# A fused two-block transformer kernel in fp32: the modulation products handed out differently between VectorE and TensorE

## Chip, cores, metric

One core of one Trainium2 chip runs the whole program. The metric is the device time of one execution in microseconds (us). A profiled execution gives the trace from which all rows below are taken.

## What is computed

The reference runs two blocks, one after the other, on x of 256 tokens by 2048 channels, all in fp32. In outline:

```
c_act = silu(c)
for l in 0, 1:                                         # first block
    shift, scale, gate = split(c_act @ w_mod[l] + b_mod[l], 3)
    h = x * (1 + scale) + shift
    l == 0:  y = diff_attention(h)                     # 8 heads
    l == 1:  k, v, F = shared_kv(x * (1 + scale_kv) + shift_kv)   # from c_act @ w_mod_kv
             y = forgetting_attention(h, k, v, F)      # 16 heads
    x = layer_norm(alpha * x + gate * y)
# second block: S5 mixer, then a squared-ReLU MLP of 8192
sh1, sc1, gt1, sh2, sc2, gt2 = split(silu(c_2) @ w_mod_2 + b_mod_2, 6)
csh1, csc1, ... = split(silu(c_ctx_2) @ w_mod_2 + b_mod_2, 6)
h_ctx, h_lat = modulate(rmsnorm(ctx), csh1, csc1), modulate(rmsnorm(x), sh1, sc1)
y = glu(gelu(s5_two_directions(h_ctx -> initial state, h_lat)))
x = x + gt1 * rmsnorm(y)
x = x + gt2 * rmsnorm(relu(modulate(rmsnorm(x), sh2, sc2) @ w1)**2 @ w2)
```

The products c @ w_mod are the subject here: a vector times a matrix of 2048 rows and 2048 columns per shift, scale or gate. All their weights are read once.

## The kernel before

**Big products.** Activations lie transposed (channels on the partitions). A weight block of 2048 by 128, called a unit here, comes in two halves of 0.5 MB; ScalarE rounds each half to `wh` (L134) and VectorE subtracts to get the rest `wl` (L135). A unit is then 48 matmuls on TensorE: `pj` in `mm_t` (L163 to L165), `pjv` in `mm_n` (L200 to L202). The MLP uses `mm_w` with 32 matmuls (L176, L177). `weights()` hands out one unit, and prepares two ahead.

**Modulation products.** `gemv` (L207) splits each 2048 by 2048 product into two halves of the columns and each half into eight chunks. A chunk is two loads `graw` of 512 KB (L268, on SP's queue, four buffers). It is used in one of two ways. On VectorE ("dve") each load is multiplied by its 128 values of c and added to the accumulator `gacc` (L237; the first load of a half by ScalarE, L235), and at the end of the half four matmuls L246 sum the partitions. On TensorE ("pe") a chunk is eight small matmuls into `g` (L222), which the trace shows as 16 records. Both ends go through L249 to L257. Products for two vectors at once (`mc`) always go to TensorE.

**Who decides.** The chunks wait in one list: m0 (layer 0), mk (keys and values), m1 (layer 1), mc (shift and scale of the S5 layer, for c_2 and the context), m1_2, m2_2 (S5's gate), m2_4, m2_3, m2_5 (MLP). Each call of `weights()` calls `bg()`, which takes the next entry of the stage's policy: "dve", "pe" or None. The policies are `P_L0A` (heads 0 to 3 of layer 0), `POL0` (heads 4 to 7), `P_ON0` (its output product), `P_KV`, `P_QG` (queries and gates of layer 1), `P_ON1` (its output product), `P_GLU`, `P_MLP`. Besides, `BG_M` chunks go to TensorE ahead of the S5 scan and `BG_V` after each of the first `BG_B` S5 blocks. Where an accumulator is still open at the start of the S5 layer, its half is finished on VectorE:

```
        while self.open:
            self.bg(1, "dve")
            self.bg_use(0)
```

`start_ctx` starts the states of the context (`ctx_states`, tile `ctx_ws`) as soon as mc is done; they are a side job in steps between units.

**Order on each engine.** A list scheduler writes the order of each engine from the program's order and its own model of the engines, so that an instruction can stand earlier than in the code when its input is expected early. On the chip each engine keeps that order. So a chunk asked for in the MLP can stand in VectorE's row ahead of the MLP's own inputs. Those inputs are `residual` (L1599, L1600), `xn` (L1612) and the split of `h` (L420), from which TensorE's first MLP matmuls start; four MLP units run interleaved there as the 16 pieces of `h` come. The keys' stage begins in the same way with `norm` (L1112, L1113) and the split `kL` (L420).

Of the kernel before, what the change touches and what calls it, by code (L numbers as in the profile page):

```python
# [47 lines left out]
KO_J = 4  # L48
KO_K = 8
P_START = ("pe",)  # L50
P_L0A = ('dve', 'pe')
P_KV = ('dve', 'pe')
P_QG = ('dve', 'dve', 'pe')
P_W = ("pe",)
P_GLU = ('dve',)
P_MLP = ('dve', None, None)
P_ON0 = ('dve', 'dve', 'dve', None)
P_ON1 = ('pe', 'dve', None)
BG_V = 5
BG_W = 0  # L60
PF_N = 6
ZT = 'm'
# [11 lines left out]
DVE_V = 3  # L74
POOL_V = tuple(range(5))
BG_M = 12
BG_B = 0
TL = True
KTS = 1
ENG = {'m0': 'dve', 'mc': 'pe', 'mk': 'dve', 'm1': 'dve', 'm2': 'pe'}  # L80
HOLD = 0
E_K = "x"
X_GLU = (0,)
X_KV = (0,)
# [5 lines left out]
X_QG = (0,)  # L90
# [16 lines left out]
class K:  # L107
# [185 lines left out]
    def bg(self, n=1, eng=None):  # L293

        for _ in range(n):
            e = eng or next(self.pol)
            if e and self.bgq and not (self.hold and self.bgq[0][0].startswith("m2")):
                name, gen, left = self.bgq[0]
                use = gen.send(ENG[name[:2]] if e == "x" else e)
                self.late.append((name, use))  # L300
                self.bg_use(LATE)
                self.bgq[0] = (name, gen, left - 1)
                if left == 1:
                    self.bgq.pop(0)
# [397 lines left out]
    def run(self):  # L702
        tc, I = self.tc, self.I
        from contextlib import ExitStack
        with ExitStack() as es:
# [21 lines left out]
            self.late = []  # L727
            self.hold = HOLD
            self.steps = itertools.cycle((1,))
# [46 lines left out]
    def V(self, n):  # L776
        i = VEC[n] * KT
        return self.vecs[:, i:i + KT]
# [112 lines left out]
    def layer0(self):  # L891
# [73 lines left out]
        self.side.append(gen)  # L965
        self.policy(P_L0A, X_L0A)
        prev = None
# [150 lines left out]
    def layer1(self):  # L1118
# [52 lines left out]
        kT, v = [], []  # L1171
        self.policy(P_KV, X_KV)
        vgen = self.s5_outputs_table(self.act.tile([128, 4096], F32, name="gen2_ws", tag="act"))
# [74 lines left out]
        def start_ctx():  # L1248
            if self.ctx is None and not self.bg_open("mc_0") and not self.bg_open("mc_1"):
                Sc, Bc = self.small_bg("sc", V("mixpre"), self.mc[1], None, self.mc[0])  # L1250
                self.ctx = self.ctx_states(Sc, Bc)
                self.side.append(self.ctx)
                self.steps = itertools.cycle(P_CTX)

        self.ctx = None
        self.policy(P_QG, X_QG)
        for h in range(16):
            start_ctx()
            ps = self.mm_t(h_)
            nc.scalar.mul(qT, ps, QS)  # L1260
            if h:
                trans()
            ps = self.mm_t(h_)
            if h:
                pv(h - 1)
            t = self.tmp("tg1")
            nc.scalar.activation(t, ps, AF.Tanh, scale=0.5)
            nc.vector.scalar_tensor_tensor(sg, t, 1.0, ps, op0=ADD, op1=MUL)
            scores(h)
        trans()  # L1270
        pv(15)
        for n in ("mc_1", "mc_0", "m1_2"):
            self.bg_finish(n)
        start_ctx()
        self.policy(P_ON1, X_ON1)
        self.norm, self.rb = self.out_norm(lambda kt: o[kt], self.m1[2], 1, rms=True)
# [69 lines left out]
    def s5_mix(self):  # L1346
# [106 lines left out]
        def open_sums(kt, z):  # L1453

            w = self.raw.tile([128, 2 * KO_J, 128], F32, name="wko", tag="raw")
            nc.sync.dma_start(w.rearrange("p j c -> p (j c)"), I["glu0"][kt])
            for j in range(KO_J):
                if kt == 0:
                    ko.append(self.pj.tile([128, 2, T], F32, name="ko", tag="pj"))
                for i in range(2):  # L1460
                    nc.tensor.matmul(ko[j][:, i], w[:, 2 * j + i], z, start=kt == 0 and i == 0, stop=False)
# [3 lines left out]
        for n, b in enumerate(blocks):  # L1465
# [66 lines left out]
            for kt, zh in late:  # L1532
                open_sums(kt, zh)
            if n < BG_B:
                self.bg(BG_V)

# [227 lines left out]
```

## Time and profile before

| what | value |
|---|---|
| median of 3 runs | 2542.77 us (2542.32 to 2544.66) |
| the profiled execution | 2548.22 us, span 2546.4 us |
| instructions | 47968 |
| mean granted TensorE clock | 0.964 of full speed |

The span is what the trace shows; the profiled execution lasts 1.82 us longer than its span. The profiled execution is 5.45 us above the median, so differences in time are worked out within the trace and then set on the median.

### The profile page before, as it was taken

The page shows a single profiled execution, that of the slowest core. Times are in us where ns is not written, and L with a number is a line of the kernel's source. Part 1 is how long each engine was busy: PE and PEld are TensorE (multiplying, and loading weights), DVE is VectorE, ACT ScalarE, POOL GpSimd, SP SyncE. Part 2 cuts the span into 40 slices and gives each one's busy share as a digit, 9 for nine tenths or more (in the row PEclk, how much of TensorE's full clock was granted, in tenths as well). Part 3 has the DMA queues.
Part 4 walks back from the last instruction along what each step waited for, and adds up shares of the span by engine and source line. Part 5 has one row for each costly group of instructions (what it writes and reads, how often), then busy time and mean ns, then how long its engine had stood idle before and what let it go on. Part 6 is the DMA issues. An engine that isn't in the chain of part 4 may idle for free.

```text
span 2546.4 us, 47968 instructions
## 1 busy us (share of the span) xinstructions
PE 2377.1 (93%) x18854; PEld 2051.9 (81%) x18854; DVE 1776.8 (70%) x3360; ACT 1239.5 (49%) x2153; POOL 118.8 (5%) x234
## 2 busy tenths in 40 slices
PE   5699999999899999999998874999899999999997
PEld 1299999999678888988886663898688888888885
DVE  3288778877775555778788997877854565665655
ACT  0554554444365556666653543544544443443442
POOL 0000000000002110000000021000000000000000
PEclk9999999999889999999998886999899999999998
DMA  9999999878769998878786762998366666666652
GB/s 325 339 344 325 323 321 344 306 275 316 265 226 342 327 332 290 296 248 290 257 273 230 233 210 77 334 320 279 118 186 187 186 187 191 189 190 184 189 182 91
DMA packets 203316, 644.66 MB, mean 253 GB/s; under 512 B 41009, under 2 KB 49457, under 8 KB 202705
## 3 DMA queue, kind: packets, MB, share of 16 engines
q1 hardware_dynamic: 195616, 620.47, 72.7%
q0 software_dynamic: 7472, 21.11, 2.1%
q8 instruction: 148, 2.42, 0.4%
q14 instruction: 80, 0.65, 0.1%
HBM read 613.71 MB, written 25.69 MB: 251 GB/s over the span
## 4 chain that ended last, share of the span: by engine, by line
PE 84%; DVE 9%; DMA 3%; ACT 2%; issue 1%; SPq 0%; POOL 0%; DVEq 0%; ACTq 0%; POOLq 0%
PE pj L176 18%; PE pj L163 12%; PE pj L164 12%; PE pj L165 12%; PE pj L177 9%; PE g L222 3%; PE pjv L200 3%; DMA graw<-in_w_mod 3%; PE pjv L201 2%; PE pjv L202 2%; DVE scan_t L1415 2%; DVE scan_t L1417 2%; DVE S L1419 2%; PE inc L697 2%; PE st L370 1%
## 5 line engine op out<-in xcount | busy, mean ns | idle before, releaser
L135 DVE TENSOR_TENSOR wl<-w,wh 128x1024 fp32r<-128x1024 f32 x631 | 770.0, 1224 | 465.2 <-ACT wh L134 457.2
L134 ACT CAST wh<-w 128x1024 fp32r<-128x1024 f32 x632 | 659.1, 1050 | 711.1 <-PE pj L176 283.0
L176 PE MATMUL pj<-h,wh 128*128 128x512 f32 x1024 | 362.9, 399 | 6.8 <-DVE h L420 5.0
L176 PE MATMUL pj<-d,wh 128*128 128x512 f32 x1024 | 360.3, 398 | 0.0
L237 DVE SCALAR_TENSOR_TENSOR gacc<-graw,csilu,gacc 128x1024 f32<-128x1024 f32 x211 | 270.2, 1281 | 27.4 <-DMA graw<-in_w_mod 18.6
L177 PE MATMUL pj<-h,wl 128*128 128x256 f32 x1024 | 287.5, 281 | 1.1 <-DVE wl L135 1.1
L177 PE MATMUL pj<-d,wl 128*128 128x256 f32 x1024 | 285.8, 280 | 0.0
L176 PEld LDWEIGHTS pj<-h,wh 128*128 128x128 f32 x1024 | 193.1, 189 | 55.8 <-issue 4.0
L176 PEld LDWEIGHTS pj<-d,wh 128*128 128x128 f32 x1024 | 192.0, 188 | 48.2 <-PE pj L177 1.7
L163 PE MATMUL pj<-hH,wh 128*128 128x256 f32 x768 | 221.6, 289 | 6.2 <-ACT hH L419 4.0
L165 PE MATMUL pj<-hH,wl 128*128 128x256 f32 x768 | 221.4, 289 | 0.5 <-DVE wl L135 0.5
L164 PE MATMUL pj<-hL,wh 128*128 128x256 f32 x768 | 221.1, 288 | 0.0
L222 PE MATMUL g<-graw,czc 128*32 128x256 f32 x1744 | 168.4, 469 | 49.6 <-DMA graw<-in_w_mod 48.0
L177 PEld LDWEIGHTS pj<-h,wl 128*128 128x128 f32 x1024 | 194.0, 189 | 1.5 <-DVE wl L135 1.5
L177 PEld LDWEIGHTS pj<-d,wl 128*128 128x128 f32 x1024 | 193.1, 189 | 0.4
L163 PEld LDWEIGHTS pj<-hH,wh 128*128 128x128 f32 x768 | 148.8, 194 | 9.8 <-ACT hH L419 4.1
L165 PEld LDWEIGHTS pj<-hH,wl 128*128 128x128 f32 x768 | 148.6, 194 | 4.5 <-issue 3.3
L164 PEld LDWEIGHTS pj<-hL,wh 128*128 128x128 f32 x768 | 148.9, 194 | 3.8 <-issue 3.7
L222 PEld LDWEIGHTS g<-graw,czc 128*32 128x32 f32 x1744 | 46.0, 119 | 129.4 <-DMA graw<-in_w_mod 105.5
L163 PE MATMUL pj<-h1H,wh 128*128 128x256 f32 x512 | 147.1, 290 | 0.3 <-ACT ctx_ws L1323 0.2
L164 PE MATMUL pj<-h1L,wh 128*128 128x256 f32 x512 | 146.4, 287 | 0.0
L165 PE MATMUL pj<-h1H,wl 128*128 128x256 f32 x512 | 146.0, 286 | 0.0
(480 smaller groups left out, 5201.4 us busy)
## 6 DMA issues: line engine op xcount, KB each, us to landing
graw<-in_w_mod SPq DMA_DIRECT2D x384, 512.0 KB, 5.8
w<-in_mlp_in SPq DMA_DIRECT2D x128, 512.0 KB, 4.3
w<-in_mlp_out SPq DMA_DIRECT2D x128, 512.0 KB, 4.3
w<-in_a_in SPq DMA_DIRECT2D x96, 512.0 KB, 6.3
graw<-in_w_kvmod SPq DMA_DIRECT2D x64, 512.0 KB, 6.6
w<-in_b_in SPq DMA_DIRECT2D x64, 512.0 KB, 5.8
w<-in_glu SPq DMA_DIRECT2D x56, 512.0 KB, 5.3
w<-in_a_v SPq DMA_DIRECT2D x32, 512.0 KB, 5.9
```

The source lines that it names most:

```text
L134: nc.scalar.copy(h, src)
L135: (eng or (nc.gpsimd if next(self.spl) else nc.vector)).tensor_sub(l, src, h)
L163: self.nc.tensor.matmul(ps, h, aH, start=kt == order[0] and not opened, stop=False)
L164: self.nc.tensor.matmul(ps, h, aL, start=False, stop=False)
L165: self.nc.tensor.matmul(ps, l, aH, start=False, stop=kt == order[-1] and last)
L176: self.nc.tensor.matmul(ps, h, view(aH, 0, [[T, 2], [1, T]]), start=kt == order[0], stop=False)
L177: self.nc.tensor.matmul(ps[:, 0], l, aH, start=False, stop=kt == order[-1])
L200: self.nc.tensor.matmul(ps[:, i], aH[:, s], h, start=half == 0 and i == 0 and k == 0, stop=False)
L201: self.nc.tensor.matmul(ps[:, i], aH[:, s], l, start=False, stop=False)
L202: self.nc.tensor.matmul(ps[:, i], aL[:, s], h, start=False, stop=half == 1 and i == 1 and k == 7)
L222: nc.tensor.matmul(st["g"][32 * q:32 * q + 32], self.cz[c][:, ch * 2 + s], raw[s][:, q * 256:q * 256 + 256], start=st["n"] == 0, stop=ch = ...
L237: nc.vector.scalar_tensor_tensor(acc, raw[s], cc, acc, op0=MUL, op1=ADD)
```

## The change

The policies are new. Layer 0's first heads and the keys' stage use no "pe" entry any more; `P_QG` starts with entries of two chunks ("twos"), a form that `bg()` now knows, until `start_ctx` switches to `P_QG2`; `P_ON1` is empty; with `HOLD` = 1 the chunks m2_* wait until the S5 layer begins; two chunks each go to TensorE after the first four S5 blocks.

```diff
-P_L0A = ('dve', 'pe')
-P_KV = ('dve', 'pe')
-P_QG = ('dve', 'dve', 'pe')
+P_L0A = ('dve', 'dve', 'dve', None)
+P_KV = ('dve',)
+P_QG = (('pe', 'pe'), 'pe')
+P_QG2 = ('dve', 'dve', None)
...
-P_ON1 = ('pe', 'dve', None)
-BG_V = 5
+P_ON1 = (None,)
+BG_V = 2
...
-BG_B = 0
+BG_B = 4
...
-HOLD = 0
+HOLD = 1
...
             e = eng or next(self.pol)
-            if e and self.bgq and not (self.hold and self.bgq[0][0].startswith("m2")):
+            for e in e if isinstance(e, tuple) else (e,):
+                if not e or not self.bgq or self.hold and self.bgq[0][0].startswith("m2"):
+                    continue
                 name, gen, left = self.bgq[0]
                 use = gen.send(ENG[name[:2]] if e == "x" else e)
                 self.late.append((name, use))
...
                 self.side.append(self.ctx)
                 self.steps = itertools.cycle(P_CTX)
+                self.policy(P_QG2, X_QG)
```

Counted over the whole program, the order has 872 rows of L222 before and 680 after (24 chunks fewer on TensorE), 211 and 260 rows of L237, 76 and 72 of L246. The loads are the same. By stage the chunks stand so:

| stage | before | after |
|---|---|---|
| heads 0 to 3 of layer 0 | 16 dve, 16 pe | 24 dve |
| heads 4 to 7; output product; ahead of the keys | 24; 12; 6 dve | the same |
| keys and values | 3 dve, 29 pe | 14 dve, 18 pe |
| queries and gates | 18 dve, 14 pe | 15 dve, 15 pe |
| output product of layer 1 | 5 dve, 6 pe | none |
| head of the S5 layer | 3 dve | none |
| S5 scan and blocks | 12 pe | 20 pe |
| GLU | 28 dve | 32 dve |
| MLP | none | 12 dve |

In the rows below, lines of the changed kernel are larger by 1 (from line 54 on), 3 (from 303) or 4 (from 1260).

**TensorE, heads 0 to 3 of layer 0**, near the end of a product's half, before: `pj` is a unit's product, `g` the modulation product (from `graw` a chunk, from `gacc` the sum at the end).

```order
L164 MATMUL pj<-hL,wh_1_3015 128x256
L165 MATMUL pj<-hH,wl_1_3016 128x256
L163 MATMUL pj<-hH,wh_1_3015 128x256
L222 MATMUL g<-graw,czc 32x256 x4
L246 MATMUL g<-gacc,one_139 32x256 x4
L164 MATMUL pj<-hL,wh_1_3015 128x256
```

TensorE at the end of such a half, after (`rb` and `sc` belong to the attention):

```order
L165 MATMUL pj<-hL,wh_0_2912 128x256
L346 MATMUL rb<-idn,ry 128x128 x2
L912 MATMUL sc<-attn_ws 128x128 x2
L247 MATMUL g<-gacc,one_139 32x256 x4
L166 MATMUL pj<-hH,wl_0_2913 128x256
```

The rows of `g` from `graw` are gone from here: between the first head's start and head 4, 148 rows of L222 become 24, all 24 at the very start; the sums of `gacc` stay.

**VectorE, start of the keys' stage**, from the middle of `norm` and `kL` on, before (`vprod` and `gen_ws` belong to a table for the S5 layer):

```order
L420 TENSOR_TENSOR kL<-u,kH 128x256
L554 TENSOR_TENSOR vprod<-gen_ws 128x512
L555 TENSOR_TENSOR vprod<-gen_ws 128x512
L1113 TENSOR_TENSOR xres<-xres,lnb 128x256
L1112 TENSOR_TENSOR xres<-xres,lnb 128x256
L420 TENSOR_TENSOR kL<-u,kH 128x256
L635 TENSOR_TENSOR gen_ws<-vprod 128x32x16
```

The same place after:

```order
L423 TENSOR_TENSOR kL<-u,kH 128x256
L557 TENSOR_TENSOR vprod<-gen_ws 128x512
L558 TENSOR_TENSOR vprod<-gen_ws 128x512
L238 SCALAR_TENSOR_TENSOR gacc<-graw,csilu,gacc 128x1024
L1116 TENSOR_TENSOR xres<-xres,lnb 128x256
L1115 TENSOR_TENSOR xres<-xres,lnb 128x256
L423 TENSOR_TENSOR kL<-u,kH 128x256
L638 TENSOR_TENSOR gen_ws<-vprod 128x32x16
```

A chunk's step on `gacc` stands between `kL` steps all the way: from the first `norm` to the last `kL` there are 15 of them, where 7 stood.

**VectorE, end of the GLU and start of the MLP**, around the last small statistics (`rq`, `ry`, `rr`) and the first inputs, before:

```order
L333 SCALAR_TENSOR_TENSOR rq<-rq 128x2
L334 SCALAR_TENSOR_TENSOR ry<-rq,ry 128x2
L1594 COPY rr<-ry 128x2
L1599 SCALAR_TENSOR_TENSOR U<-U,gs_18449,rrb 128x256
L1600 TENSOR_TENSOR xres<-xres,U 128x256
L1612 TENSOR_TENSOR xn<-xres,rrb 128x256
```

The same place after:

```order
L336 SCALAR_TENSOR_TENSOR rq<-rq 128x2
L337 SCALAR_TENSOR_TENSOR ry<-rq,ry 128x2
L238 SCALAR_TENSOR_TENSOR gacc<-graw,csilu,gacc 128x1024
L1598 COPY rr<-ry 128x2
L238 SCALAR_TENSOR_TENSOR gacc<-graw,csilu,gacc 128x1024
L1603 SCALAR_TENSOR_TENSOR U<-U,gs_18176,rrb 128x256
L238 SCALAR_TENSOR_TENSOR gacc<-graw,csilu,gacc 128x1024
L1604 TENSOR_TENSOR xres<-xres,U 128x256
L238 SCALAR_TENSOR_TENSOR gacc<-graw,csilu,gacc 128x1024
L1616 TENSOR_TENSOR xn<-xres,rrb 128x256
```

Steps on `gacc` now stand in the stretch in which the MLP's inputs are made: from the last `xy` (L1578) to the last `h` (L420) there are 27, 8 of them ahead of the first L1599, where none stood; the rest of the MLP has none.

## Rows read from the trace of the kernel before

**Rows 1.** The page: span, and each engine's busy time with its share and count.

```profile
span 2546.4 us, 47968 instructions
PE 2377.1 (93%) x18854; PEld 2051.9 (81%) x18854; DVE 1776.8 (70%) x3360; ACT 1239.5 (49%) x2153; POOL 118.8 (5%) x234
```

**Rows 2.** Windows by stage: stretch, length, busy per engine, clock, DMA share, GB/s.

```profile
112.00:362.00 250.00, 244.86 (x2083) 225.36 (x2084) 197.57 (x307) 128.68 (x232) 17.93 (x38) 0.99 0.94 335
362.00:569.00 207.00, 207.00 (x1738) 204.24 (x1737) 165.32 (x242) 98.82 (x164) 3.71 (x8) 1.00 0.87 311
...
698.00:963.00 265.00, 258.17 (x2546) 225.88 (x2549) 169.03 (x257) 148.29 (x284) 40.62 (x89) 0.96 0.89 305
963.00:1242.00 279.00, 278.30 (x2426) 245.47 (x2418) 206.38 (x363) 184.33 (x381) 8.80 (x18) 0.99 0.83 280
1242.00:1374.00 132.00, 130.67 (x1161) 113.38 (x1161) 102.36 (x187) 65.52 (x118) 2.44 (x6) 1.00 0.78 260
...
1620.00:1777.00 157.00, 157.00 (x1267) 142.98 (x1262) 121.37 (x119) 77.63 (x125) 3.86 (x6) 1.00 0.88 309
1777.00:1820.00 43.00, 30.37 (x143) 23.39 (x142) 34.78 (x97) 21.97 (x40) 0.00 (x0) 0.80 0.27 86
1820.00:2524.00 704.00, 702.44 (x4008) 607.90 (x4006) 415.72 (x550) 306.02 (x406) 0.00 (x0) 1.00 0.60 182
```

**Rows 3.** Chain in 112 to 362 us: start, length, instruction, repetitions.

```profile
147.67 1.00 PE g L222 x16
...
158.56 0.57 PE g L222 x8
```

**Rows 4.** Groups by line in 112 to 362 us: count, busy, mean ns, idle before.

```profile
L237 DVE SCALAR_TENSOR_TENSOR gacc<-graw,csilu,gacc 128x1024 f32<-128x1024 f32 x27 | 34.5, 1279 | 0.0
...
L222 PE MATMUL g<-graw,czc 128*32 128x256 f32 x272 | 21.5, 391 | 0.0
L594 PE MATMUL wps<-idn,gen_ws 128*128 128x128 f32 x124 | 19.0, 273 | 0.0
```

**Rows 5.** The same view in 362 to 569 us.

```profile
L237 DVE SCALAR_TENSOR_TENSOR gacc<-graw,csilu,gacc 128x1024 f32<-128x1024 f32 x47 | 60.2, 1282 | 0.9 <-ACT gacc L235 0.7
```

**Rows 6.** VectorE's timeline at the keys' start: start, length, instruction [idle before, releaser].

```profile
714.02 1.29 DVE L237 SCALAR_TENSOR_TENSOR gacc<-graw,csilu,gacc 128x1024 f32<-128x1024 f32 x1
715.22 0.43 DVE L1113 TENSOR_TENSOR xres<-xres,lnb 128x256 f32<-128x256 f32 x1
...
732.18 0.76 DVE L420 TENSOR_TENSOR kL<-u,kH 128x256 fp32r<-128x256 f32 x2 [0.17 <-ACT kH L419]
```

**Rows 7.** Windows of tile `inc` alone (PE, PEld, DVE, ACT; clock, DMA, GB/s).

```profile
1242.00:1374.00 132.00, 12.88 (x192) 10.71 (x192) 0.00 (x0) 6.54 (x12) 1.00 0.78 260
```

**Rows 8.** VectorE's timeline at the S5 layer's head.

```profile
1375.35 1.28 DVE L237 SCALAR_TENSOR_TENSOR gacc<-graw,csilu,gacc 128x1024 f32<-128x1024 f32 x1
...
1378.09 0.15 DVE L1090 TENSOR_SCALAR mr<-sums 128x2 f32<-128x2 f32 x1
1378.21 0.21 DVE L1340 TENSOR_TENSOR ctx_ws<-ctx_ws 128x32 f32<-128x32 f32 x1
...
1382.51 0.42 DVE L1112 TENSOR_TENSOR xres<-xres,lnb 128x256 f32<-128x256 f32 x1 [0.19 <-PE lnb L343]
```

**Rows 9.** TensorE's timeline at the end of the S5 scan.

```profile
1569.06 1.97 PE L1487 MATMUL y<-vl,sn 128*64 128x64 f32 x32 [24.66 <-ACT sn L1482]
```

**Rows 10.** VectorE's timeline from the last `xy` to the last `h`.

```profile
1779.91 0.42 DVE L1578 TENSOR_TENSOR xy<-xres,U 128x256 f32<-128x256 f32 x1
...
1783.44 0.16 DVE L385 TENSOR_SCALAR var<-ysum 128x2 f32<-128x2 f32 x1 [2.95 <-PE ysum L380]
...
1789.32 0.48 DVE L1599 SCALAR_TENSOR_TENSOR U<-U,gs,rrb 128x256 f32<-128x256 f32 x1 [1.31 <-PE rrb L343]
...
1819.30 0.42 DVE L420 TENSOR_TENSOR h<-u,h 128x256 fp32r<-128x256 f32 x1 [0.77 <-ACT h L419]
```

**Rows 11.** TensorE's timeline: the first MLP matmul.

```profile
1792.96 0.77 PE L176 MATMUL pj<-h,wh 128*128 128x512 f32 x1 [3.69 <-DVE h L420]
```

## The prediction

> **What bounds the kernel now.** The page first: TensorE is busy for 93% of the span, VectorE for 70% [rows 1]. That mean hides the stages, so the windows by stage come next [rows 2]. From 112 to 1374 us and in the GLU TensorE is busy nearly all the time, and what counts there is how much TensorE has to do. VectorE is busy there for 197.6 of 250 us with heads 0 to 3, where the DMA engines stand at 0.94 too. The row that matters most is 1777 to 1820 us: TensorE is busy for 30.4 of 43 us at a clock of 0.80, VectorE for 34.8, the DMA engines for 0.27. There VectorE makes the MLP's inputs: its timeline goes from the first L1599 at 1789.32 to the last `h` at 1819.30 with no idle time but the 0.77 us in front of that `h` [rows 10], and TensorE's first MLP matmul waits for `h` [rows 11]. So in this kernel a chunk on VectorE is cheap or dear by the stage in which it stands, and so is a chunk on TensorE.
>
> **Prices.** A chunk on TensorE in one piece is 1.00 us of the chain, half a chunk 0.57 [rows 3]; one cut in two thus costs 1.14. A step on `gacc` lasts 1.28 us, but the next instruction starts 1.20 us after it [rows 6]; a chunk is two steps, 2.4 us.
>
> **Heads 0 to 3.** Gone from TensorE are 124 of 148 rows of L222. The chain of before has 31 pieces of 0.57 us here, 17.7 us; all records of L222 in the window have 21.5 us [rows 4]. VectorE gets about 20 steps more, if it does what it did with heads 4 to 7 (47 steps against 27, [rows 4, 5]): 20 by 1.28 is 25.6 us on top of 197.6, so 223 us. Bounds of the gain: heads 4 to 7 have the same units and already the policy that heads 0 to 3 now get, and took 207 us against 250 [rows 2], but heads 0 to 3 keep most of the generator's matmuls `wps` (19.0 us, [rows 4]): 43 less 19 is 24 at best. At worst TensorE waits for `wl`, since VectorE at 223 us of some 230 is nearly full and its steps stand in one row: then 4 us are left. I take 17, nearer to the best, because the loads get lighter too (eight chunks of 1 MB fewer in a stage with the DMA engines at 0.94), which helps each unit. **−17 (−24 to −4).**
>
> **Keys and values.** VectorE has 15 steps instead of 7 between the first `norm` and the last `kL`. This stretch ends at 732.9 us without an idle time worth the name [rows 6], and TensorE's first four units of keys run at the pace of `kL`: 8 by 1.20 is +9.6. The keys' units lose 96 rows of L222, 12 chunks by 1.00, −12. Together −2.4 (−7 to +9: at worst the DMA engines, at 0.89 over the whole stage [rows 2], give back the gain). The values keep 17 chunks, now in halves: 17 by 0.14 is **+2.4** (0 to +4).
>
> **Queries and gates.** The twos put 64 more rows of L222 into the first ten units, 8 chunks by 1.14, +9.1; after `start_ctx` there are 48 fewer, −6.0. TensorE is busy for 278.3 of 279 us, so both count: **+3.1** (0 to +8; above it if the four `graw` buffers make TensorE wait for a load, for which the windows leave little reason, the DMA engines being at 0.83).
>
> **Output product of layer 1.** 52 rows of L222 fewer, −6.5. Sixteen rows of `inc` slip in from the context's states, which start later: 32 records at 12.88/192 = 0.067 us [rows 7] are +2.1. **−4.4** (−8 to −2).
>
> **S5 layer.** The three open chunks are gone, of which one step or two stood in the chain of the layer norm (1375.35 us, [rows 8]): −1.2. In their place the rest of the context's last block, 23 small operations, stands between L1090 and the first L1112, where before one `ctx_ws` step was left (0.21 us, [rows 8]). 23 by 0.2 to 0.3 is 6 us, of which some falls into waits of the chain for TensorE: +3.7. **+2.5** (0 to +5). The eight chunks more on TensorE after the blocks have cover: TensorE waits 24.66 us for the end of the scan [rows 9], and eight chunks, even at twice 1.00 us, are 16. Taken at 0 (−2 to +6); without that cover they would cost the 8 to 16 us.
>
> **GLU.** Four chunks more on VectorE, 4 by 2.4 us, in a stage where it is busy for 121.4 of 157 and TensorE for all of it: hidden, but one more half has its four sums: **+1** (0 to +3).
>
> **Start of the MLP.** The twelve chunks that the policy asks for in the MLP do not spread over its 700 us, where VectorE has room (415.7 of 704, [rows 2]); in the order they stand in front, 27 steps from the last `xy` to the last `h`. Nineteen lie between the first L1599 and the last `h`, on an engine that was never idle there: 19 by 1.20 is 22.8. Eight lie in the chain of small statistics, 9.6 us, of which the waits for `ysum` (2.95) and `rrb` (1.31) can cover one step each: 7.2 is seen. That makes 30. TensorE cannot use the time, because all units at hand need the same `h`. I take **+28** for 1 to 2 us that TensorE's backlog gives back at the end (before, its four interleaved units ended after the last `h`). Bounds: 20, if the first eight are all covered and the backlog gives 3; 31, if no wait covers more than one step. The 24 loads find idle DMA engines (0.27): 12 MB at the 335 GB/s of heads 0 to 3 are 38 us, less than the 60 us over which they are used. The rest of the MLP stays as it is, since TensorE is its bound and has the same matmuls.
>
> **Sum.** −17 −2.4 +2.4 +3.1 −4.4 +2.5 +1 +28 = +13.2 us. The profiled execution of 2548.22 us would become 2561.4, and as it lies 5.45 us above the median of the runs, the median would go from 2542.77 to **2556 us**, 0.5% more.
>
> **Rivals.**
> *VectorE has room, and TensorE's relief shows everywhere (faster).* For it: 24 chunks leave TensorE, the engine with the highest share. If the steps at the MLP's start cost nothing, the sum is −14.8, so 2528 us. It decides where the MLP's start costs less than 14.8 us, that is, when fewer than 13 of the 27 steps are seen. Against it: the 30 us without a gap [rows 10]. The Trainium skill (Perfetto Trace Analysis, Identifying the Most-Contended Engine) says that the engine with the highest occupancy is to be relieved first; by that alone the 24 chunks at 1.00 us would give −24, some 2519 us. The rows of heads 0 to 3 agree with that rule, those of the MLP's start do not, where VectorE is the fuller one. Chance 0.16.
> *Gains and losses cancel.* Heads 0 to 3 give 24, the output product 8, and the MLP's start costs only 20: −24 −2.4 +2.4 +3.1 −8 +2.5 +1 +20 = −5.4; with heads at 20 it is about −1. About 2541. Chance 0.13.
> *VectorE becomes the bound with heads 0 to 3.* `wl` comes late, the stage gains 4 instead of 17: +26, 2569 us. For it: 223 us of work in a row of steps of 1.2 us. Against it: `wl` is made two units ahead. Chance 0.13.
> *The forecast*: 0.58, by itself 2548 to 2565.
>
> A measurement of this kernel can tell about 0.2% (5 us) from no change. Faster by over that 0.16, within it 0.14, slower 0.70. The range of 8 in 10 reaches from 2536, which leaves out the lower part of the first rival, to 2570, which takes in the third.
>
> **What would show it.** In the profile of the changed kernel: from the first L1603 to the last `h` (L423) some 52 us instead of 30, with VectorE full; heads 0 to 3 in about 233 us with VectorE above 0.9; the last `kL` some 9 us later after the first `norm`; no `g` in the output product of layer 1; the wait ahead of the last S5 blocks shorter by what the eight chunks take, and its end where it was. The prediction is wrong if VectorE's steps at the MLP's start wait for nothing and still TensorE's matmuls come no later, or if heads 0 to 3 lose more than 24 us.

## The result and the profile after

The changed kernel takes 2580.74 us (median of 4 runs, 2577.93 to 2583.97), the kernel before 2542.55 us (4 runs): ratio 1.0146, 95% interval 1.0133 to 1.0158. It is slower, as forecast, but by 38 us where 13 were forecast.

The page of the changed kernel, the lines that answer to [rows 1]:

```profile
span 2580.7 us, 47306 instructions
PE 2359.9 (91%) x18462; PEld 2044.8 (79%) x18462; DVE 1826.9 (71%) x3409; ACT 1241.1 (48%) x2152; POOL 126.9 (5%) x234
```

TensorE is busy for 17 us less (2377.1 before, [rows 1]) and still ends 34 us later: it waits more. Where it does so is read from the windows by stage of the changed kernel (columns as in [rows 2]; heads 0 to 3, heads 4 to 7, keys, values, queries and gates, output product of layer 1, end of the GLU to the first MLP units):

```profile
115.60:341.50 225.90, 219.73 (x1803) 214.71 (x1804) 199.83 (x282) 124.46 (x212) 17.89 (x32) 0.97 0.92 332
341.50:558.30 216.80, 211.26 (x1752) 208.92 (x1750) 179.43 (x283) 104.61 (x181) 7.62 (x12) 0.98 0.81 296
...
687.20:819.30 132.10, 121.47 (x1026) 112.53 (x1027) 114.94 (x171) 81.05 (x155) 18.75 (x36) 0.88 0.81 275
819.30:948.30 129.00, 124.61 (x1267) 105.90 (x1265) 69.77 (x92) 64.15 (x119) 20.12 (x41) 0.99 0.94 333
948.30:1248.70 300.40, 287.37 (x2480) 250.26 (x2480) 210.09 (x375) 181.64 (x376) 10.89 (x28) 0.97 0.78 258
1248.70:1371.00 122.30, 122.30 (x1060) 109.04 (x1060) 81.06 (x156) 67.11 (x125) 4.67 (x7) 1.00 0.58 183
...
1782.30:1840.00 57.70, 25.38 (x90) 16.21 (x91) 54.34 (x99) 17.21 (x32) 1.56 (x2) 0.62 0.83 276
```

In the queries' stage TensorE is no longer busy throughout: 287.4 of 300.4 us where it was 278.3 of 279 [rows 2]. In the last row VectorE is nearly full (54.3 of 57.7 us) and TensorE less than half.

The stages of both kernels, each from the first matmul of its kind in the trace to the first of the next one (us; the columns of e1 to e12 are the experiments below). S5 begins where the output product of layer 1 ends, the GLU with its first matmul, the start of the MLP where the GLU's last matmul ends; it runs to the first matmul on `d`, the rest of the MLP to the last one. The changed kernel, e1 and e2 are the same program up to the end of the GLU: there their stages differ by up to 2 us, the start by 4.2. That is how far a single trace can be trusted.

| stage | before | after | e1 | e2 | e3 | e4 | e5 | e6 | e7 | e8 | e9 | e10 | e11 | e12 |
|---|---|---|---|---|---|---|---|---|---|---|---|---|---|---|
| start | 112.2 | 115.6 | 113.8 | 111.4 | 114.0 | 111.3 | 113.4 | 112.7 | 114.4 | 112.8 | 115.2 | 112.1 | 111.3 | 114.8 |
| layer 0, heads | 456.9 | 442.6 | 443.6 | 442.6 | 443.6 | 443.6 | 443.4 | 447.9 | 444.6 | 448.7 | 443.3 | 448.9 | 447.7 | 448.4 |
| its output product | 129.0 | 129.0 | 127.9 | 129.0 | 127.9 | 127.9 | 129.0 | 127.9 | 130.1 | 126.4 | 125.7 | 128.1 | 125.7 | 125.7 |
| keys | 143.0 | 132.1 | 132.8 | 131.6 | 132.6 | 133.3 | 132.8 | 146.2 | 153.9 | 151.7 | 113.1 | 146.4 | 114.8 | 115.2 |
| values | 122.9 | 128.9 | 128.9 | 128.9 | 128.9 | 128.9 | 128.9 | 119.8 | 125.4 | 124.9 | 153.1 | 119.8 | 158.3 | 163.8 |
| queries, gates | 277.9 | 300.4 | 300.7 | 300.9 | 276.0 | 316.9 | 295.7 | 285.2 | 289.0 | 287.8 | 307.0 | 282.7 | 285.2 | 285.4 |
| output product, layer 1 | 131.8 | 122.3 | 122.3 | 122.3 | 137.6 | 122.6 | 121.5 | 124.9 | 117.1 | 117.1 | 122.3 | 124.9 | 125.8 | 125.8 |
| S5 | 218.5 | 225.1 | 223.1 | 225.0 | 239.0 | 219.4 | 223.3 | 217.3 | 219.0 | 221.0 | 226.5 | 217.8 | 221.5 | 217.2 |
| GLU | 185.2 | 186.3 | 186.0 | 187.1 | 186.3 | 186.2 | 185.5 | 185.5 | 184.8 | 184.8 | 188.0 | 185.3 | 186.6 | 186.1 |
| start of the MLP | 113.9 | 146.4 | 121.3 | 122.9 | 144.8 | 144.8 | 144.8 | 144.8 | 120.8 | 122.7 | 145.6 | 113.0 | 117.1 | 112.1 |
| rest of the MLP | 632.6 | 629.1 | 632.5 | 639.8 | 629.1 | 629.1 | 629.1 | 629.1 | 630.3 | 630.4 | 629.1 | 630.9 | 630.4 | 630.9 |

Two stages make the loss: the queries with the output product behind them (409.7 to 422.7, +13.0) and the start of the MLP (+32.5). S5 adds 6.6, the values 6.0. Layer 0's heads give back 14.3, the keys 10.9.

The start of the MLP on VectorE's timeline after, the answer to [rows 10], and TensorE's first MLP matmul, the answer to [rows 11]:

```profile
1788.85 0.42 DVE L1582 TENSOR_TENSOR xy<-xres,U 128x256 f32<-128x256 f32 x1
...
1804.73 0.48 DVE L1603 SCALAR_TENSOR_TENSOR U<-U,gs,rrb 128x256 f32<-128x256 f32 x1
1805.13 1.28 DVE L238 SCALAR_TENSOR_TENSOR gacc<-graw,csilu,gacc 128x1024 f32<-128x1024 f32 x1
...
1856.32 0.43 DVE L423 TENSOR_TENSOR h<-u,h 128x256 fp32r<-128x256 f32 x1 [0.77 <-ACT h L422]
```

```profile
1810.95 0.79 PE L177 MATMUL pj<-h,wh 128*128 128x512 f32 x1 [6.25 <-DVE h L423]
```

From the first residual to the last `h` it is 51.6 us (30.0 before), from the last `xy` to the first residual 15.9 (9.4 before). The last `xy` itself comes 6.6 us after the GLU's last matmul at 1782.3, where it took 2.6: two steps on `gacc` stand between that matmul and it too.

The queries' stage: who TensorE waited for, after (engine, line, what; us in total, times, longest). Before, the same view has 0.6 us.

```profile
PE pj L164 <- ACT h1H L422: 4.4, 1, 4.4
PE pj L164 <- ACT ctx_ws L1327: 4.2, 1, 4.2
PE pv L1240 <- ACT ws L1236: 3.8, 2, 3.2
PE g L223 <- DMA graw<-in_w_mod: 1.7, 2, 1.3
PE inc L700 <- DVE ws L1272: 1.4, 1, 1.4
```

The waits are mostly for ScalarE, hardly for loads (the 4.4 us for `h1H` lie ahead of the stage's first matmul, at the end of the values). Around the start of the context's side job ScalarE's timeline reads so, after:

```profile
1063.77 0.80 ACT L1230 ACTIVATE ws<-ws,sr 128x128 f32<-128x128 f32 x2 [0.60 <-DVE sr L1227]
...
1064.62 1.04 ACT L135 CAST wh<-w 128x1024 fp32r<-128x1024 f32 x1
1065.57 2.29 ACT L1319 ACTIVATE ub<-uctx,ctx_ws 64x64 f32<-64x64 f32 x5
1067.77 0.46 ACT L1236 COPY ws<-tp 128x384 f32<-128x384 f32 x1
```

and TensorE's:

```profile
1064.05 0.28 PE L165 MATMUL pj<-h1L,wh 128*128 128x256 f32 x1
1064.17 0.28 PE L166 MATMUL pj<-h1H,wl 128*128 128x256 f32 x1
1064.29 0.78 PE L1235 MATMUL tp<-idn,ws 128*128 128x128 f32 x3
1068.28 0.49 PE L1240 MATMUL pv<-ws,v 128*128 128x128 f32 x2 [3.21 <-ACT ws L1236]
...
1075.52 0.41 PE L165 MATMUL pj<-h1L,wh 128*128 128x256 f32 x1
1075.73 0.41 PE L166 MATMUL pj<-h1H,wl 128*128 128x256 f32 x1
```

TensorE has turned the attention's weights (`tp`) and needs them copied (L1236) for `pv`; five copies of the side job (`ub`) and a cast stand in front of that copy in ScalarE's row. And some of what comes after the gap runs slower: matmuls of the same kind start 0.12 us apart before it (1064.05, 1064.17) and 0.21 us apart behind it (1075.52, 1075.73). Windows of 4 us show TensorE's granted clock (the first number of the last three): 1.00 up to 1068 us, then 0.65, then 0.50, which is the lower of its two levels, 1.2 GHz in place of 2.4, and 1.00 again from 1076 us on.

```profile
1064.00:1068.00 4.00, 1.00 (x6) 0.56 (x6) 2.21 (x2) 3.90 (x10) 0.00 (x0) 1.00 0.98 354
...
1072.00:1076.00 4.00, 4.00 (x35) 3.67 (x33) 2.91 (x7) 3.52 (x10) 0.00 (x0) 0.50 0.66 244
```

Ahead of the wait of 4.2 us for `ctx_ws` ScalarE's row is again taken up by the side job, eight copies `ub` and the copies of its sums:

```profile
1128.91 1.77 ACT L1319 ACTIVATE ub<-uctx,ctx_ws 64x64 f32<-64x64 f32 x4
...
1131.21 1.77 ACT L1319 ACTIVATE ub<-uctx,ctx_ws 64x64 f32<-64x64 f32 x4
1133.01 1.07 ACT L1327 COPY ctx_ws<-inc 128x512 f32<-128x512 f32 x2
```

ScalarE as a whole is not full: it is busy for 181.6 of 300.4 us, 184.3 of 279 before [rows 2]. What TensorE waits for in these two places stands behind the side job in its row.

### The profile page after: what moved, and what is told of

Read it like the earlier page. It is cut to its first block, busy times and chain, and to the rows that moved or that the text cites. A ratio compares the mean times of both kernels' runs of the same rounds, so it can differ in the third digit from the quotient of the medians.

```text
span 2580.7 us, 47306 instructions
## 1 busy us (share of the span) xinstructions
PE 2359.9 (91%) x18462; PEld 2044.8 (79%) x18462; DVE 1826.9 (71%) x3409; ACT 1241.1 (48%) x2152; POOL 126.9 (5%) x234
## 4 chain that ended last, share of the span: by engine, by line
PE 77%; DVE 12%; DMA 4%; ACT 4%; issue 2%; SPq 0%; POOL 0%; DVEq 0%; ACTq 0%; POOLq 0%
PE pj L177 18%; PE pj L164 11%; PE pj L165 11%; PE pj L166 11%; PE pj L178 9%; DMA graw<-in_w_mod 3%; PE pjv L203 2%; PE pjv L201 2%; PE pjv L202 2%; DVE scan_t L1419 2%; DVE scan_t L1421 2%; PE g L223 2%; DVE S L1423 2%; PE inc L700 1%; DVE gacc L238 1%
## 5 line engine op out<-in xcount | busy, mean ns | idle before, releaser
L238 DVE SCALAR_TENSOR_TENSOR gacc<-graw,csilu,gacc 128x1024 f32<-128x1024 f32 x260 | 333.4, 1282 | 22.1 <-ACT gacc L236 11.7
L178 PE MATMUL pj<-h,wl 128*128 128x256 f32 x1024 | 289.0, 282 | 2.1 <-DVE wl L136 2.1
L223 PE MATMUL g<-graw,czc 128*32 128x256 f32 x1360 | 138.7, 494 | 58.0 <-DMA graw<-in_w_mod 56.6
L223 PEld LDWEIGHTS g<-graw,czc 128*32 128x32 f32 x1360 | 33.2, 122 | 130.0 <-DMA graw<-in_w_mod 115.8
```

The source lines that it names most:

```text
L178: self.nc.tensor.matmul(ps[:, 0], l, aH, start=False, stop=kt == order[-1])
L223: nc.tensor.matmul(st["g"][32 * q:32 * q + 32], self.cz[c][:, ch * 2 + s], raw[s][:, q * 256:q * 256 + 256], start=st["n"] == 0, stop=ch = ...
L238: nc.vector.scalar_tensor_tensor(acc, raw[s], cc, acc, op0=MUL, op1=ADD)
```

## Experiments

The short edits are to the changed kernel. Where no interval is given, the time is that of a single run.

**e1: the MLP's chunks behind the last `h`.** `after` is set to the last subtraction of `affine_split` when the MLP begins; nothing is left out.

```diff
...
-                        nc.vector.scalar_tensor_tensor(acc, raw[s], cc, acc, op0=MUL, op1=ADD)
+                        with self.tc.issue_after(self.after) if self.after else contextlib.nullcontext():
+                            nc.vector.scalar_tensor_tensor(acc, raw[s], cc, acc, op0=MUL, op1=ADD)
...
-            nc.vector.tensor_sub(aL, u, aH)
+            self.last_h = nc.vector.tensor_sub(aL, u, aH).ins
...
         self.policy(P_MLP, X_MLP)
+        self.after = self.last_h
```

> The changed kernel, with the steps on gacc that belong to the MLP's chunks queued on VectorE behind the last h; loads and all else as in the changed kernel. Theory A (the MLP's start lost 32 us because 27 steps on gacc stand ahead of and between its inputs): the time from the end of the GLU to the first matmul on d falls from 146 us to about 114 us, the whole to about 2548 us. Rival B (it is the 24 loads or the low clock there that cost the time, the steps only stand where waiting is anyway): the stretch stays above 130 us, the whole above 2565 us.

2556.79 us, ratio to the kernel before 1.0058 (1.0039 to 1.0077). The start of the MLP falls from 146.4 to 121.3 us. VectorE's timeline of e1 shows the last `h` 29.9 us after the first residual (1796.20) again, and the steps behind it:

```profile
1826.10 0.43 DVE L427 TENSOR_TENSOR h<-u,h 128x256 fp32r<-128x256 f32 x1 [0.77 <-ACT h L426]
1826.44 2.60 DVE L242 SCALAR_TENSOR_TENSOR gacc<-graw,csilu,gacc 128x1024 f32<-128x1024 f32 x2
```

Theory A holds for 25 of 32 us, rival B falls. The 7 us left are the GLU's own chunks: their steps stand ahead of the last `xy` and in the statistics, outside the edge.

**e2: the MLP's chunks on TensorE.**

```diff
-P_MLP = ('dve', None, None)
+P_MLP = ('pe', None, None)
```

> The changed kernel with the MLP's twelve chunks on TensorE instead of VectorE. Theory A: VectorE's stretch between the first residual and the last h is 30 us again, the start of the MLP gets back about 30 us, and TensorE pays up to 8 us for chunks among the MLP's matmuls and about 2 us at the end: whole about 2555 us. Rival B (loads or clock): no more than 10 us come back.

2565.79 us. The start of the MLP is 122.9 us, so 23.5 come back: less than the 30 of theory A, as in e1, but far above the 10 of rival B. The rest of the MLP is 10.7 us longer, where 8 were allowed for.

**e3 and e4: one, or two, chunks per unit in the queries' stage.**

```diff
-P_QG = (('pe', 'pe'), 'pe')
+P_QG = ('pe',)            # e3
+P_QG = (('pe', 'pe'),)    # e4
```

> The changed kernel with one chunk per unit instead of two and one in turn in the queries' stage. Theory C (the stage's 18 us come from the context's side job starting later and its ScalarE copies standing ahead of the attention's): the job starts later still, TensorE's idle time in the stage stays at 8 us or more, the stage at 290 us or more, and the head of the S5 layer does not get shorter. Rival D (the twos cost it: TensorE waits for loads, matmuls cut in pieces): idle under 4 us, the stage about 282 us.

> The changed kernel with two chunks in every unit of the queries' stage until the context's products are done, so that the side job starts about two heads earlier than with one per unit. Theory C: idle time of TensorE in the stage under 6 us, the stage about 285 us, and the S5 layer's head shorter by 3 us. Rival D (twos): more waits for loads, the stage at 296 us or more.

2583.96 and 2588.21 us. In the stage itself rival D is right: 276.0 us with one, 300.4 with one and a half, 316.9 with two. But what e3 wins is lost behind: the context's side job starts later, the output product takes 137.6 us and S5 239.0. Queries, output product and S5 together: 652.6 (e3), 647.8 (changed), 658.9 (e4), 628.2 before. Neither theory C nor D accounts for the loss: the number per unit only moves it. The side job's first matmul (`sf`) comes 146.1 us after the stage's first matmul in e3 and 109.4 us after it in e4, so some two heads earlier, as expected; but the changed kernel has 114.5, so against that e4 gains only 5 us, since its units are so much longer. The kernel before has 72.4.

**e5: a third of m1_2's chunks back on TensorE.**

```diff
-P_QG2 = ('dve', 'dve', None)
+P_QG2 = ('dve', 'dve', 'pe')
```

> The changed kernel with a third of the chunks of m1_2 on TensorE again after the context's products are done (dve, dve, pe in the queries' stage, as in the kernel before). Theory F (in the units beside the context's side job TensorE waits for ScalarE, and chunks on TensorE only filled that wait): five to eight chunks more on TensorE cost under 3 us, idle time there falls from 11 us, queries and output product together stay at 420 to 426 us. Rival G (TensorE is the bound there, the idle time is an accident of the order): they get longer by 1 us per chunk, 428 us or more.

2571.54 us. Five chunks more are done on TensorE (368 records of `g` in queries and output product, 288 in the changed kernel), and queries with output product take 417.2 us instead of 422.7: shorter, not longer. TensorE's waits in e5's queries' stage:

```profile
PE pj L164 <- ACT h1H L422: 4.4, 1, 4.4
PE pv L1240 <- ACT ws L1236: 3.2, 1, 3.2
PE g L223 <- DMA graw<-in_w_mod: 1.2, 2, 1.0
```

The wait for `ctx_ws` is gone, that for `ws` once in place of twice. Theory F holds, rival G falls: TensorE does 6.8 us more on `g` (29.5 against 22.7) and the pair of stages is 5.5 us shorter, more than the traces of one program differ. Here TensorE had time, and work taken off it came back as waiting.

**e6: every fourth chunk of heads 0 to 3 on TensorE.** Eight chunks are done there that the change pushes into later stages.

```diff
-P_L0A = ('dve', 'dve', 'dve', None)
+P_L0A = ('dve', 'dve', 'dve', 'pe')
```

> The changed kernel with every fourth chunk of heads 0 to 3 on TensorE in place of a free turn, so that eight chunks are done there and no longer pushed into the later stages. Theory H (the loss in the queries' stage comes from those eight chunks: they delay the context's products, put twos of chunks beside the attention and start the side job late): layer 0 costs 7 to 10 us more (about 451 us), the keys gain less, but queries and output product together come back from 423 to about 410 us and the S5 layer to about 220 us. Rival C2 (the loss lies in the policy of the queries' stage itself): they stay above 418 us.

2565.43 us. Layer 0's heads 447.9 (+5.3 against the changed kernel, so 0.66 us per chunk), queries with output product 410.1 (−12.6), S5 217.3 (−7.8). What theory H forecast came: queries, output product and S5 together are at 627.4, where the kernel before has 628.2. The side job starts 59.8 us after the stage's first matmul. The keys lose 14.1 and the values gain 9.1. The windows of queries and output product with the instructions on `g` alone, of the kernel before, of the changed one and of e6, and last the whole of e6:

```profile
964.10:1373.70 409.60, 28.52 (x339) 9.72 (x342) 1.85 (x5) 1.00 0.81 273
```

```profile
948.30:1371.00 422.70, 22.74 (x288) 6.34 (x288) 1.48 (x4) 0.98 0.72 236
```

```profile
954.60:1364.60 410.00, 16.55 (x192) 4.48 (x192) 1.11 (x3) 0.98 0.69 223
```

```profile
954.60:1364.60 410.00, 398.73 (x3438) 354.95 (x3439) 288.17 (x540) 247.53 (x495) 11.94 (x26) 0.98 0.69 223
```

So the time of this pair of stages divides up as follows (us):

| TensorE in queries, gates and output product | before | after | e5 | e6 |
|---|---|---|---|---|
| idle | 2.0 | 13.0 | 5.2 | 11.3 |
| on `g` | 28.5 | 22.7 | 29.5 | 16.6 |
| on all else | 379.1 | 386.9 | 382.5 | 382.2 |
| granted clock | 1.00 | 0.98 | 0.98 | 0.98 |

Two things follow. Against the kernel before, TensorE has 12 us less of `g` to do in e6, in the same time: idle time takes up 9 of them, the slower rest of the work 3. And of what e6 gets back against the changed kernel, 6.2 us are chunks that TensorE no longer does in this pair, 4.7 lie in the rest of its work, and less than 2 in its waits.

The waits do not vanish: TensorE waits 9.0 us for ScalarE in another place (`tp` for L1230). The longer of the two is not ScalarE's alone. The rows of ScalarE, VectorE and TensorE there:

```profile
1128.94 3.58 ACT L1319 ACTIVATE ub<-uctx,ctx_ws 64x64 f32<-64x64 f32 x8 [1.41 <-PE inc L700]
...
1136.62 0.80 ACT L1230 ACTIVATE ws<-ws,sr 128x128 f32<-128x128 f32 x2 [3.08 <-DVE sr L1227]
```

```profile
1135.23 1.28 DVE L238 SCALAR_TENSOR_TENSOR gacc<-graw,csilu,gacc 128x1024 f32<-128x1024 f32 x1 [2.77 <-DMA graw<-in_w_mod]
1136.43 0.15 DVE L1227 RECIPROCAL sr<-se 128x2 f32<-128x2 f32 x1
```

```profile
1137.07 1.09 PE L1235 MATMUL tp<-idn,ws 128*128 128x128 f32 x3 [7.53 <-ACT ws L1230]
```

First eight copies of the side job stand in ScalarE's row; then ScalarE waits 3.08 us itself, for `sr` on VectorE, and `sr` stands behind a step on `gacc` that waits 2.77 us for its load. The view names the engine whose wait ended last; here a chunk on VectorE and its load were behind it.

**e7 and e8: attempts to beat both.** Both have the edge of e1, one chunk per S5 block and `P_QG = ('pe',)`, `P_ON0 = ('dve',)`; e7 also has `POL0 = ('dve',)`, e8 instead the `P_L0A` of e6.

> The changed kernel with VectorE taking a chunk in every unit of heads 4 to 7 and of layer 0's output product, one chunk per unit on TensorE in the queries' stage, one per S5 block, and the MLP's chunks on VectorE behind the last h. If VectorE has room in heads 4 to 7 (165 of 207 us busy before) and the eight pushed chunks are what costs time later: about 2520 us, faster than both. If VectorE becomes the bound in layer 0, that layer takes 455 us or more and the whole is about 2540 us.

> As the kernel with VectorE in every unit of heads 4 to 7, but those heads as in the changed kernel and instead every fourth chunk of heads 0 to 3 on TensorE. By the price of a chunk on TensorE it should be about 8 us slower than that one in layer 0 if VectorE has room in heads 4 to 7, and faster if not: about 2525 us.

2553.73 us, ratio 1.0036 (1.0023 to 1.0049), and 2550.51 us, 1.0023 (1.0014 to 1.0033). Both miss. VectorE had room in layer 0 (444.6 us in e7), so the 455 us feared there did not come; but with the m1 chunks done earlier the keys' units have mc on TensorE, and the keys take 153.9 and 151.7 us (keys and values together 279.4 and 276.6, 265.9 before). Queries, output product and S5 are at 625.0 and 625.9: e7 does the pushed chunks early too, on VectorE in heads 4 to 7, and the loss there is gone as in e6 (its policies for the later stages differ too).

**e9: the keys' steps behind the last `kL`.** Without the edge of the MLP; the lines of e1 in `gemv` and `affine_split` stand as there.

```diff
         self.affine_split(self.norm, S, B, k_)
+        self.after = self.last_h
```

> The changed kernel with every step on gacc from the keys' stage on queued on VectorE behind the last kL, so that none of the 15 stands between the first norm and the last kL. If these steps cost the keys' stage their length (15 by 1.20 us, 10 us of which are the change's): the last kL comes 18 us sooner after the first norm (29 us instead of 47), and the keys take 120 us or less instead of 132, unless the loads then bound them. If TensorE's units there have slack against VectorE: the keys stay within 4 us of 132.

2592.56 us. The last `kL` ends 28.8 us after the first `norm`, as expected (682.07 to 710.9 us), and the keys take 113.1 instead of 132.1: the steps did cost that. But the values take 153.1 instead of 128.9. e9's windows over the keys and the values, and TensorE's waits in the values:

```profile
684.30:797.40 113.10, 109.37 (x940) 103.66 (x941) 99.60 (x137) 72.59 (x130) 8.39 (x15) 0.97 0.81 287
797.40:950.50 153.10, 134.46 (x1361) 110.91 (x1360) 99.22 (x135) 73.38 (x147) 30.81 (x62) 0.89 0.95 346
```

```profile
PE g L226 <- DMA graw<-in_w_mod: 7.8, 9, 3.3
PE kps L656 <- DMA gen_ws<-d_b: 5.6, 1, 5.6
```

Keys and values together are 266.2 us (261.0 in the changed kernel, 265.9 before, 266.0 in e6). In the second stretch the DMA engines are at 0.95, move some 53 MB (346 GB/s over 153.1 us; the changed kernel some 43 MB, 333 over 129.0), and TensorE, with the same 256 records of `g` there, waits for `graw` and for the generator's transfer at a granted clock of 0.89: the gain of the first stretch is given back in waiting for loads. The queries take 307.0 us on top of that, which was not followed.

**e10: a version from the parts that won.** `P_L0A` of e6, the edge of e1, and

```diff
-P_GLU = ('dve',)
+P_GLU = ('dve',) * 28 + (None,) * 4
```

> Every fourth chunk of heads 0 to 3 on TensorE, the MLP's chunks behind the last h, and no chunk in the last four units of the GLU. From the stages of the earlier runs: 688.5 us up to the keys, 893 from the keys to the S5 layer, 955 from the GLU on, whole about 2538 us, a little faster than the kernel before.

2536.58 us (10 runs), ratio 0.998 (0.9969 to 0.9991): faster than the kernel before by 0.2%, and 44 us faster than the changed one. The start of the MLP is 113.0 us, 113.9 before; e11 and e12 with the same lines have 117.1 and 112.1. So most of the 7 us that e1 left were the GLU's last chunks; e8, with e1's edge and e6's `P_L0A` but chunks in those units, has 122.7.

**e11 and e12: the same with e9's edge in the keys' stage; and that with e5's policy.**

> The same with the steps on gacc behind the last kL in the keys' stage as well: if those steps are on the path there, 10 to 18 us less in the keys' stage, whole about 2525 us; if not, as without it.

> The same again, with a third of the chunks of m1_2 on TensorE in the queries' stage. If TensorE waits for ScalarE beside the context's side job (theory F), this is free or gives 2 to 5 us; if TensorE is the bound there, 5 us more.

2553.33 us, ratio 1.003 (1.0017 to 1.0042), and 2548.31 us, 1.0012 (0.9999 to 1.0024). e11 misses in part for the reason that e9 shows (keys 114.8, values 158.3, together 7 us more than in e10); the rest is spread over the stages behind and was not followed. The policy of e5 neither costs nor gives in the queries here (285.4 against 285.2), with four chunks more on TensorE (240 records against 176): free, as theory F allows, but without the gain that e5 had there. The 5 us between the medians of e11 and e12 do not show in their traces, whose spans are 2547.0 and 2547.7 us.

## Why the prediction was wrong

The direction and the largest cause were right: the start of the MLP was forecast to lose 28 us, and it lost 32.5. But the time is 24.7 us above the 2556 of the forecast and above its range. In the traces the stages came to +34.2 us where 13.2 were summed. Queries and output product are 14.3 above their terms, the start of the MLP 4.5, S5 4.1, the values 3.6, layer 0's heads 2.7; the keys are 8.5 below. The first of these comes from a wrong step; the others are in the main terms of the wrong size.

**Queries, gates and the output product: the step that failed.** The prediction summed +3.1 (0 to +8) and −4.4, with the sentence that TensorE is busy for 278.3 of 279 us, "so both count". Measured: +22.5 and −9.5, together +13.0. A TensorE that is busy throughout was read as a TensorE that alone sets the time: only its work on `g` was priced, and waits for another engine were put at nothing. The work on `g` did fall, by 5.8 us. But idle time rose by 11.0, and the rest of TensorE's work took 7.8 us longer. That TensorE's work alone does not set the time is shown twice: e5 puts chunks back and the pair gets 5.5 us shorter; e6 has 12 us less of `g` than the kernel before and the pair is as long (410.0 and 409.6). The list of what is late next ended at the loads (the four `graw` buffers), for which TensorE waited 1.7 us; it should have followed the attention's chain through ScalarE's row, which holds the side job's copies too, and through VectorE's, where the chunks' steps stand (e6). What brought the loss here is the eight chunks that heads 0 to 3 no longer do: with them back (e6) 12.6 us come back in the pair and 7.8 in S5, about half of the 12.6 because TensorE has fewer chunks there. That their return frees the stages is shown; why one order of the rows brings longer waits than another is not, and e3 and e4 show that the number of chunks per unit is no handle on it.

Part of the 13.0 is the clock: the granted clock of the queries' stage is 0.97, where it was 0.99 [rows 2], and the two rows at 1075.52 show matmuls at the lower level, where the windows have 0.50. The Trainium skill (TensorE: Matmul & The Clock Gate, HAM oscillation) says that gaps in TensorE's work make the matmuls behind them run cold; the trace agrees, 0.21 us in place of 0.12. So a wait here costs more than its own length, which the prediction's prices left out.

**Start of the MLP, +28: right in its mechanism, measured +32.5.** From residual to last `h` it is 21.6 longer (22.8 less what was taken off), in the statistics 6.5 (7.2). The 4 us not foreseen lie ahead of the last `xy`: steps of the GLU's own last chunks. The prediction counted the GLU's chunks as hidden behind TensorE, which is true of all but those beside the last units. e1 and e10 settle it.

**S5, +2.5: measured +6.6.** The context's work ends 13.6 us after the output product in the changed kernel, 5.0 before. e4 and e6, in which it is done ahead of S5, have 219.4 and 217.3, so it is the rest of the context's work, at about twice the size taken. The eight chunks more on TensorE had the cover that was counted on: its wait at the end of the scan is 7.1 us shorter than before [rows 9], and e6, with the same chunks there, is below the 218.5 of before.

```profile
1573.76 1.55 PE L1491 MATMUL y<-vl,sn 128*64 128x64 f32 x24 [17.58 <-ACT sn L1486]
```

**Heads 0 to 3, −17: measured −24.1**, the "best" bound (225.9 against 250.0 us, [rows 2]). VectorE did not become the bound: TensorE waited for `wl` for 1.0 us in all. But heads 4 to 7, left out of the sum, took 216.8 instead of 207.0: TensorE waits once for 5.5 us for a row statistic (`ry`) on VectorE, and 23 records of the generator's `wps`, 4.0 us, ran there, where none did before. So a few of the 24.1 us only moved. Together −14.3; that this is near the 17 is in part luck.

**Keys, −2.4: measured −10.9; values, +2.4: measured +6.0.** The 9.6 us on VectorE were right: from the first `norm` (685.18) to the end of the last `kL` (732.2) it is 47.0 us, 36.9 before. But they were charged in full to TensorE, which used most of them: in the longer stretch it did more. The windows of the stretch, the changed kernel's and then the one of before, show 199 and 141 matmuls, and TensorE idle for 10.4 us against 6.8, so only about 3.5 us were lost:

```profile
687.00:735.00 48.00, 37.65 (x199) 33.70 (x200) 45.00 (x78) 22.77 (x46) 1.99 (x5) 0.68 0.75 244
```

```profile
698.00:733.00 35.00, 28.17 (x141) 25.59 (x142) 34.78 (x70) 20.44 (x42) 1.65 (x3) 0.66 0.64 199
```

The values lose the 4.4 us for `h1H`, a wait for ScalarE again; it is 0.4 us in e6.

**GLU, +1:** +1.1. **Not in the sum:** the start is 3.4 us longer, as it varies from 111.3 to 115.6 us among the kernels above, which do not differ there; the rest of the MLP is 3.5 shorter.

**The last step, setting the difference on the median:** the trace of before lay 5.45 us above the median used there, 5.67 above the one of the four runs (2542.55), that of the changed kernel 1.69 (2582.43 against 2580.74). So of the 38.2 us between the medians 34.2 are in the traces, and 4 lie in which execution was profiled.

**The rivals.** That TensorE's relief shows everywhere was true of layer 0's heads, and of keys and values together by 4.9 us. The third rival, VectorE as the bound of heads 0 to 3, did not come, though VectorE stood at 199.8 of 225.9 us. A loss by waits in the queries' stage was in none.

## What to carry to other kernels

An engine that is busy all the time need not be what sets the time: work taken off it can turn into waiting (12 us of matmuls removed, no gain). So ask for each stage which chain through the other engines ends next, and price the gain only up to it. Busy shares do not name that chain: ScalarE, at which these waits ended, was busy for some 0.6 of these stages (247.5 of 410.0 us in e6); what counted was what stood in its row in front of the copy needed. When work is spread by turns, follow what the turns not used push into later stages: eight chunks left out early cost 20 us in the queries, the output product and S5, against the 5 us that they saved in the heads and 5 in keys and values. And where a scheduler writes the order, "in the MLP" can mean in front of the MLP, as it did here: filler on an engine that keeps its order needs an explicit edge behind the inputs that the stage waits for, which here gave 25 us for a few lines.

## What was not expected of the hardware

The first matmul on layer 0's first weights came between 111.3 and 115.6 us in the thirteen traces of the changed kernel and its variants, whose program is the same up to there: about 4 us of difference in a stage before anything was changed, as much as some of the terms above. And in e9's values the DMA engines moved 346 GB/s, against 335 in the fullest stage of the kernel before, with TensorE waiting for single transfers all the same.
